# The last layer's output projection as seven-product 2x2 block products

## The chip, the cores and the metric

The kernel runs on one core of a Trainium2 chip. What counts is the time of one execution on the device, in microseconds (us); of several runs the median is given. In the profile the engines are PE (TensorE, the matmuls), DVE (VectorE), ACT (ScalarE), POOL (GpSimd) and SP, which issues the DMAs; PEclk is the clock granted to TensorE, 1.00 being full speed. Each engine carries out its instructions in the order of its own queue.

## The reference

Two encoder layers over 1024 positions of width 1024, all in float32. Only the end of a layer matters here:

```python
y_a = (o_a * jax.nn.silu(z_a)) @ w_attn_proj[l]
y_f = (_fourier_branch(u_f) * jax.nn.silu(z_f)) @ w_fourier_proj[l]
m = (jax.nn.sigmoid(g_a + b_merge[l, 0]) * y_a
     + jax.nn.sigmoid(g_f + b_merge[l, 1]) * y_f)
x = x + m @ w_out[l]
```

The attention branch has 512 channels (`o_a`), `m` and `x` have 1024.

## The kernel before

Activations lie with features on the 128 partitions and the 1024 positions along the free axis, eight tiles of 128 features each. A float32 product is made of three products of a shorter type (`F32R`): every operand is split into an upper part (a copy, rounded) and a lower part (the difference), and upper x upper, upper x lower and lower x upper are added up in PSUM. So a tile of an output of 1024 positions with eight input tiles takes 8 x 2 x 3 = 48 matmuls of 512 columns (`fm`, `mm3`), one with four input tiles 24. Weights are loaded and split on POOL in `wtile` and `split_pool` (L131 the upper, L132 the lower part); activations are split with ACT making the upper and DVE the lower part.

A layer ends with `merge`. Four tiles `og` (what goes into `w_attn_proj`) are loaded and split into `oG` (ACT L797, DVE L798). Then eight tiles t follow: the gate logits `sa` are loaded and put through the sigmoid (ACT L802), the Fourier side's finished summand `mfl` is loaded into one of the three staging buffers (`stage`), TensorE makes `ya` with 24 matmuls, DVE multiplies it from PSUM with the gate (L805) and adds the summand (L806), and ACT L807 and DVE L808 split the sum into the two parts of `mT`. The output projection follows: eight tiles `xo` of 48 matmuls (L165 to L167; in the first tile, where the last tile of `mT` comes late, L187 to L189), DVE adds the residual (L821) and SP stores (L822). The last output tile is added and stored in two halves.

A scheduler sets the order in which each engine's instructions stand, from the order of the code and from estimates; waits are semaphores. PSUM holds two buffers of 1024 columns for the results of `fm`: a tile of `ya` or `xo` can begin when the result two tiles earlier has been read.

## Time and profile before

| | us |
|---|---|
| median of three runs | 1683.38 (1680.42 to 1683.61) |
| the profiled execution | 1679.84 |
| its span (first to last event of the trace) | 1678.1 |
| PE busy | 1647.2 (98%) |
| DVE, ACT, POOL busy | 829.2, 657.6, 730.1 |
| last layer: ya products, output projection | 1541 to 1586, 1586 to 1674 |

The profiled execution is 1.74 us longer than its span and lies below the median of the runs. Busy shares are means over the whole span; what a stage is worth is read from the stage alone, by windows of the trace, and from what ended the waits of the engine that sets its end.

### The profile page before, as it was taken

To read this page: it belongs to the slowest core of one execution; us is meant where nothing else is said; L and a number is where in the kernel's file an instruction comes from. 1 tells how busy PE (TensorE), PEld (TensorE's weight loads), DVE (VectorE), ACT (ScalarE), POOL (GpSimd) and SP (SyncE) were. 2 spreads that over 40 slices of the span, in tenths; PEclk is the share of its full clock that TensorE was granted. 3 is DMA by queue.
4 is the path that set the end of the run, shared out by engine and by line. 5 is a ranking of instruction groups with operands and counts; after the bars stand their busy time and mean duration, and the time that the engine had idled before them with its cause. 6 is when DMAs were issued, how large, how long until landed. Compare 5 with 4: busy or idle time off the path is not lost.

```text
span 1678.1 us, 22508 instructions
## 1 busy us (share of the span) xinstructions
PE 1647.2 (98%) x8374; PEld 1344.1 (80%) x8374; DVE 829.2 (49%) x1358; ACT 657.6 (39%) x1257; POOL 730.1 (44%) x575
## 2 busy tenths in 40 slices
PE   7999999999999999999999999999999999999998
PEld 5888889887777777778878888898777777777887
DVE  7643452334666665465334535424356666654711
ACT  4322321327666666432112223213277666652300
POOL 5622361474454553443254324525644554433531
PEclk9999999999999999999999999999999999999999
DMA  5302330355555553374342023213544555534741
GB/s 193 132 13 71 91 125 32 126 182 186 169 176 199 176 188 132 132 239 162 126 157 63 13 78 121 101 57 132 194 161 176 198 189 176 176 120 173 238 147 75
DMA packets 118366, 234.76 MB, mean 140 GB/s; under 512 B 27888, under 2 KB 48624, under 8 KB 118000
## 3 DMA queue, kind: packets, MB, share of 16 engines
q1 hardware_dynamic: 117904, 228.59, 39.4%
q0 software_dynamic: 352, 4.73, 0.7%
q8 instruction: 66, 1.08, 0.3%
q14 instruction: 44, 0.36, 0.1%
HBM read 116.89 MB, written 49.28 MB: 99 GB/s over the span
## 4 chain that ended last, share of the span: by engine, by line
PE 85%; DMA 4%; issue 3%; DVE 3%; POOL 2%; ACT 2%; SPq 0%; DVEq 0%; POOLq 0%; ACTq 0%
PE pt L714 4%; PE s L165 4%; PE o L718 3%; PE gf L167 3%; PE s L167 3%; PE gf L165 3%; PE xo L167 3%; PE gf L166 3%; PE xo L166 3%; PE xo L165 3%; PE s L166 3%; PE o L720 3%; PE ga L167 3%; PE ga L166 3%; PE ga L165 3%
## 5 line engine op out<-in xcount | busy, mean ns | idle before, releaser
L693 DVE TENSOR_REDUCE nm<-s 128x1 f32<-128x512 f32 x256 | 172.6, 687 | 128.5 <-PE s L167 126.9
L700 ACT ACTIVATE E<-s,nm 128x512 f32<-128x512 f32 x256 | 173.3, 684 | 51.6 <-issue 29.2
L714 PEld LDWEIGHTS pt<-identr,P 128*128 128x128 f32 x1024 | 112.7, 141 | 40.2 <-DMA P<-E 6.8
L131 POOL TENSOR_SCALAR pT<-pf 128x512 fp32r<-128x512 f32 x96 | 59.4, 618 | 176.2 <-ACT pf L725 146.5
L132 POOL TENSOR_TENSOR pT<-pf,pT 128x512 fp32r<-128x512 f32 x96 | 123.8, 1290 | 8.0
L196 DVE TENSOR_TENSOR pT<-pt,pT 128x512 fp32r<-128x512 f32 x160 | 109.2, 684 | 31.5 <-ACT pT L195 30.1
L714 PE MATMUL pt<-identr,P 128*128 128x128 f32 x1024 | 119.9, 239 | 4.7 <-DMA P<-E 4.6
L195 ACT ACTIVATE pT<-pt 128x512 fp32r<-128x512 f32 x160 | 95.5, 598 | 46.1 <-PE pt L714 45.0
L165 PE MATMUL s<-kT,qT 96*128 96x512 f32 x256 | 110.4, 432 | 0.5
L718 PE MATMUL o<-pT,V 128*128 128x512 f32 x256 | 109.7, 428 | 0.0
L720 PE MATMUL o<-pT,V 128*128 128x512 f32 x256 | 106.5, 416 | 1.2 <-POOL pT L132 1.1
L165 PE MATMUL ga<-xg,wga_h 128*128 128x512 f32 x256 | 103.1, 403 | 0.0
L166 PE MATMUL ga<-xg,wga_h 128*128 128x512 f32 x256 | 102.0, 399 | 0.0
L167 PE MATMUL ga<-xg,wga_l 128*128 128x512 f32 x256 | 101.7, 397 | 0.0
L165 PE MATMUL gf<-xg,wgf_h 128*128 128x512 f32 x256 | 101.0, 395 | 0.0
L166 PE MATMUL s<-kT,qT 96*128 96x512 f32 x256 | 101.0, 394 | 0.0
L167 PE MATMUL gf<-xg,wgf_l 128*128 128x512 f32 x256 | 100.9, 394 | 0.0
L166 PE MATMUL gf<-xg,wgf_h 128*128 128x512 f32 x256 | 100.9, 394 | 0.0
L167 PE MATMUL s<-kT,qT 96*128 96x512 f32 x256 | 96.5, 396 | 0.0
L725 ACT ACTIVATE pf<-pt 128x512 f32<-128x512 f32 x96 | 57.4, 598 | 97.3 <-PE pt L714 92.7
L167 PE MATMUL xo<-mT,wo_l 128*128 128x512 f32 x224 | 87.9, 392 | 0.0
L166 PE MATMUL xo<-mT,wo_h 128*128 128x512 f32 x224 | 87.9, 392 | 0.0
(335 smaller groups left out, 4269.2 us busy)
## 6 DMA issues: line engine op xcount, KB each, us to landing
P<-E SPq DMA_DIRECT2D x256, 256.0 KB, 2.3
kv_d<-KV SPq DMA_DIRECT2D x16, 640.0 KB, 2.9
KVh<-kv_d SPq DMA_DIRECT2D x16, 640.0 KB, 4.9
wgf_r<-in_w_fm SPq DMA_DIRECT2D x16, 512.0 KB, 3.5
mf_d<-sgf SPq DMA_DIRECT2D x16, 512.0 KB, 3.3
wga_r<-in_w_fm SPq DMA_DIRECT2D x16, 512.0 KB, 3.6
ga_d<-sga SPq DMA_DIRECT2D x16, 512.0 KB, 3.0
sa<-ga_d SPq DMA_DIRECT2D x16, 512.0 KB, 4.1
```

Of the source, the lines that this page charges most:

```text
L131: nc.gpsimd.tensor_scalar(hi, src, 1.0, 1.0, op0=ALU.mult, op1=ALU.mult)
L132: nc.gpsimd.tensor_tensor(lo, src, f(hi), op=ALU.subtract)
L165: self.nc.tensor.matmul(out, ah, bh, start=(i == 0), stop=False)
L166: self.nc.tensor.matmul(out, ah, bl, start=False, stop=False)
L167: self.nc.tensor.matmul(out, al, bh, start=False, stop=(i == n - 1))
L195: nc.scalar.activation(hi, ps, AF.Copy)
L196: nc.vector.tensor_tensor(lo, ps, f(hi), op=ALU.subtract)
L693: nc.vector.tensor_reduce(nm2[:, kc:kc + 1], s_ps, axis=AX.X, op=ALU.max)
L700: nc.scalar.activation(e, halves[kc], AF.Exp, bias=nm, accum_out=sum_e[:, h, t, kc:kc + 1])
L714: nc.tensor.transpose(tp[:, j * P:(j + 1) * P].bitcast(F32R), u["P"][j][k // 4][:, (k % 4) * P:(k % 4 + 1) * P], self.identr)
L718: nc.tensor.matmul(u["o"], u["V"][:, kk, :], q[0], start=(u["n"] == 0), stop=False)
L720: nc.tensor.matmul(u["o"], u["V"][:, kk, :], q[1], start=False, stop=(u["n"] == ST))
```

## The change

Layer 0 keeps `merge`. The last layer gets `merge_last`, which makes the same output projection in blocks. For each pair of output tiles (j = 0 to 3) the weights are two block rows and two block columns (the input tiles 0 to 3 and 4 to 7), and the positions two halves of 512. A 2x2 block product takes eight products of blocks; here it takes seven, of sums and differences of blocks. A product of blocks is four input tiles x 3 = 12 matmuls of 512 columns, so that a pair of output tiles takes 7 x 12 = 84 matmuls instead of 96.

On the side of `m` the operands are the blocks M1 (lower half of tiles 0 to 3), M2 (tiles 4 to 7) and the mixtures XA and XB, made from tile k and tile k + 4 as soon as both are there: therefore the ya products run in the order 0, 4, 1, 5, 2, 6, 3, 7, and the weights of tiles k and k + 4 are loaded and split as one pair of 1024 columns (`pair`). The gate logits go through the three staging buffers, as the summands do (`gal`, `mfl`). The lower parts of XA and XB are issued one tile later (`tail`): XA's on DVE, XB's on POOL for k = 0 and 1 and on DVE for k = 2 and 3.

`stream` runs the 28 products. On the weights' side POOL makes four sums or differences for each j, and ACT and DVE split the operands (`split_fast`). Behind each product ACT or DVE takes the result out of PSUM or combines it with an earlier one, and POOL adds residuals (`base`). The PSUM buffers are those of a new pool (`px`), six of 512 columns, in place of the old two of 1024. The buffers for the further weight tiles (`R`) are in a pool that opens when the pool of `oG` has closed.

Lines of the changed kernel that are named below: L138 and L139 are `split_fast` (ACT, DVE), L133 and L134 `split_pool`; L875 is the multiplication of ya with the gate, L876 the addition of the summand, L879 the difference of the halves of a tile, L892 to L894 the differences with the other tile, L895 and L896 the copies to XA and XB, L897 their lower parts; L933 to L936 the four weight sums, L952 `base`, L970 to L972 the matmuls of a step, L980 the copy of a first result (`c`).

```diff
-    def merge(self, l, og3, x_ctx, res_d, out_d):
+    def merge(self, l, og3, x_ctx, res_d):
...
                 ps = self.fm_late(w, mT, f"xo{t}") if t == 0 else self.fm(w, mT, KD, f"xo{t}")
-                dst = out_d[t] if last else self.x1_d[t]
-                for cs in (slice(0, 512), slice(512, S)) if last and t == KD - 1 else (slice(0, S),):
-                    nc.vector.tensor_tensor(xr[:, cs], ps[:, cs], xr[:, cs], op=add)
-                    nc.sync.dma_start(dst[:, cs], xr[:, cs])
...
+    def merge_last(self, l, og3, x_ctx, res_d, out_d):
...
+        self.psum(f"pm{l}")
...
+        with ExitStack() as ctx:
+            mp = ctx.enter_context(tc.tile_pool(name=f"m{l}", bufs=1, side=xs))
+            sp = ctx.enter_context(tc.tile_pool(name=f"sa{l}", bufs=1, side=xs))
+            M1, M2, XA, XB = [[mp.tile([P, 4, n], F32R, name=f"{name}{j}") for j in range(2)]
+                              for name, n in (("M1", 512), ("M2", S), ("XA", S), ("XB", S))]
+            cut = lambda x, cs: [y[:, :, cs] for y in x]
+            self.X = {B11: M1, B21: cut(M2, lo), B22: cut(M2, hi), T1: cut(XA, lo), T3: cut(XA, hi), T4: cut(XB, lo), T2: cut(XB, hi)}
+            self.sa_p, self.cp = sp, None
+            mixed = {}
+            with tc.tile_pool(name=f"og{l}", bufs=1, side=os) as op_:
+                oG = [op_.tile([P, 4, S], F32R, name=f"oG{j}") for j in range(2)]
+                for t in range(4):
+                    o = self.stage(self.og_d[t], f"og{t}") if t < 3 else og3
+                    nc.scalar.activation(oG[0][:, t, :], o, AF.Copy)
+                    nc.vector.tensor_tensor(oG[1][:, t, :], o, f(oG[0][:, t, :]), op=sub)
+
+                def pair(k):
+                    raw = self.wp.tile([P, S], F32, tag="raw", name=f"wa{k}_r")
+                    w = [self.wp.tile([P, S], F32R, tag=n, name=f"wa{k}_{n}") for n in ("hi", "lo")]
+                    for j, cs in enumerate((lo, hi)):
+                        nc.sync.dma_start(raw[:, cs], io["w_ap"][l, k + 4 * j])
+                    self.split_pool(raw, *w)
+                    for j, cs in enumerate((lo, hi)):
+                        W[k + 4 * j] = [x[:, cs].rearrange("p (k m) -> p k m", k=4) for x in w]
+
+                W = {}
+                pair(0)
+                tail = []
+                for t in (0, 4, 1, 5, 2, 6, 3, 7):
+                    k = t % 4
+                    ga = self.stage(self.ga_d[t], f"gal{t}")
+                    mf = self.stage(self.mf_d[t], f"mfl{t}")
+                    ps = self.fm(W.pop(t), oG, 4, f"ya{t}")
+                    if t < 3:
+                        pair(t + 1)
+                    if t + 1 == KD:
+                        stream = self.stream(l, res_d, out_d)
+                        next(stream)
+                    nc.scalar.activation(ga, ga, AF.Sigmoid, bias=self.bm[:, l, 0, t:t + 1])
+                    sa = mixed[t] = sp.tile([P, S], F32, tag="sa", bufs=4, name=f"sa{t}")
+                    nc.vector.tensor_tensor(sa, ps, ga, op=mult)
+                    nc.vector.tensor_tensor(sa, sa, mf, op=add)
+                    if t < 4:
+                        self.split_fast(sa[:, lo], M1[0][:, k], M1[1][:, k])
+                        nc.gpsimd.tensor_tensor(sa[:, lo], sa[:, hi], sa[:, lo], op=sub)
+                    else:
+                        self.split_fast(sa, M2[0][:, k], M2[1][:, k])
+                    for do in tail:
+                        do()
+                    tail = []
+                    if t < 4:
+                        continue
+                    if t + 1 == KD:
+                        self.psum(f"px{l}")
+                        next(stream)
+                        next(stream)
+                    y = mixed[k]
+                    nc.vector.tensor_tensor(y[:, hi], sa[:, hi], y[:, hi], op=sub)
+                    nc.gpsimd.tensor_tensor(sa[:, hi], sa[:, hi], y[:, lo], op=sub)
+                    nc.gpsimd.tensor_tensor(sa[:, lo], sa[:, lo], sa[:, hi], op=sub)
+                    nc.scalar.activation(XA[0][:, k], y, AF.Copy)
+                    nc.scalar.activation(XB[0][:, k], sa, AF.Copy)
+                    low = lambda e, X, x, k: e.tensor_tensor(X[1][:, k], x, f(X[0][:, k]), op=sub)
+                    tail = [lambda k=k, y=y: low(nc.vector, XA, y, k), lambda k=k, sa=sa: low(nc.gpsimd if k < 2 else nc.vector, XB, sa, k)]
+                for do in tail:
+                    do()
+            self.cp = ctx.enter_context(tc.tile_pool(name=f"xo{l}", bufs=1, side=os))
+            for _ in stream:
+                pass
+
+    def stream(self, l, res_d, out_d):
+        nc, io = self.nc, self.io
+        add, sub = ALU.add, ALU.subtract
+        J = KD // 2
+        steps = [(0, 0), (1, 0), (0, 2), (1, 2)]
+        steps += [(j, i) for j in range(J) for i in ((1, 3, 4, 5, 6) if j < 2 else range(7))]
+        loads = [s for s in steps if s[1] < 2]
+        last = {(j, r): max(steps.index((j, i)) for i in ((0, 1, 2) if r == 0 else (1, 5))) for j in range(J) for r in range(2)}
+        R, ops, sums, banks, tiles, xr, pair = {}, {}, {}, {}, {}, {}, {}
+        early, nb = 2, 4
+
...
+        def prep(n):
+            if n >= len(steps):
+                return
+            pump(n)
+            j, i = steps[n]
+            half = lambda r, h: R[j, r][:, h * 512:h * 512 + 512]
+            if i == 1:
+                s1, s2, s3, s4 = sums[j] = [self.cp.tile([P, 512], F32, tag=f"s{m}", name=f"S{m}_{j}") for m in range(1, 5)]
+                nc.gpsimd.tensor_tensor(s1, half(1, 0), half(1, 1), op=add)
+                nc.gpsimd.tensor_tensor(s2, s1, half(0, 0), op=sub)
+                nc.gpsimd.tensor_tensor(s3, half(0, 0), half(1, 0), op=sub)
+                nc.gpsimd.tensor_tensor(s4, half(0, 1), s2, op=sub)
+            if i in (0, 2, 5):
+                src = half(i == 5, i != 0)
+            else:
+                src = sums[j][(None, 1, None, 2, 0, None, 3)[i]]
+            if n % 2 == 0:
+                pair[n] = pair[n + 1] = [self.wp.tile([P, S], F32R, tag=t, name=f"A{t}{n}") for t in ("hi", "lo")]
+            cs = slice(n % 2 * 512, n % 2 * 512 + 512)
+            ops[n] = [x[:, cs] for x in pair.pop(n)]
+            self.split_fast(src, *ops[n])
+            pump(n + 1)
+
...
+        for n in range(AHEAD):
+            prep(n)
+        yield
+        V = nc.vector
+        lo, hi = slice(0, 512), slice(512, S)
+        for n, (j, i) in enumerate(steps):
+            prep(n + AHEAD)
+            tag = ("b1", "bx", "b1", "bx", "bz", "bx", "bz")[i]
+            fresh = i in (0, 1, 4)
+            if fresh:
+                banks[j, tag] = self.ps.tile([P, 512], F32, tag=tag, bufs=2, name=f"{tag}_{j}")
+            b = banks[j, tag]
+            ah, al = ops.pop(n)
+            bh, bl = self.X[i]
+            for k in range(4):
+                ks = slice(k * P, k * P + P)
+                nc.tensor.matmul(b, ah[:, ks], bh[:, k, :], start=(fresh and k == 0), stop=False, skip_group_check=True)
+                nc.tensor.matmul(b, ah[:, ks], bl[:, k, :], start=False, stop=False, skip_group_check=True)
+                nc.tensor.matmul(b, al[:, ks], bh[:, k, :], start=False, stop=(k == 3), skip_group_check=True)
+            if i in (0, 1 if j > 1 else 2):
+                tiles[j, int(i == 0)] = self.sa_p.tile([P, S], F32, tag="sa", bufs=4, name=f"c{j}{int(i == 0)}")
+            for m in range(2):
+                if i == (((2, 1), (0, 2))[j > 1][m]):
+                    xr[j, m] = self.stage(res_d[2 * j + m], f"xr{j}{m}")
+            a, t, ra, rt = tiles.get((j, 0)), tiles[j, 1], xr.get((j, 0)), xr.get((j, 1))
+            if i == 0:
+                nc.scalar.activation(t[:, lo], b, AF.Copy)
+            elif i == 1:
+                V.tensor_tensor(a[:, hi], b, t[:, lo], op=add)
+                base(a, hi, ra)
+            elif i == 2:
+                V.tensor_tensor(a[:, lo], b, ra[:, lo], op=add)
+                store(j, 0, a, lo)
+            elif i == 3:
+                V.tensor_tensor(t[:, hi], b, t[:, lo], op=add)
+            elif i == 4:
+                V.tensor_tensor(t[:, hi], b, t[:, hi], op=add)
+                base(t, hi, rt)
+                store(j, 1, t, hi)
+            elif i == 5:
+                V.tensor_tensor(t[:, lo], b, t[:, lo], op=add)
+                base(t, lo, rt)
+                store(j, 1, t, lo)
+            else:
+                V.tensor_tensor(a[:, hi], b, a[:, hi], op=add)
+                store(j, 0, a, hi)
+            yield
 
```

The order of instructions on DVE, from the second-last pair of ya products to the last multiplication of the stage. The names are those of the code with a running number (`M11` and `M21` the lower parts of M1 and M2, `XA1` and `XB1` those of XA and XB). Before:

```order
L805 TENSOR_TENSOR sa5_14754<-ya5_14765,sa5_14754 128x1024
L806 TENSOR_TENSOR sa5_14754<-sa5_14754,mfl5_14757 128x1024
L808 TENSOR_TENSOR mT1_14539<-sa5_14754,mT0_14538 128x1024
L805 TENSOR_TENSOR sa6_14794<-ya6_14805,sa6_14794 128x1024
L806 TENSOR_TENSOR sa6_14794<-sa6_14794,mfl6_14797 128x1024
L808 TENSOR_TENSOR mT1_14539<-sa6_14794,mT0_14538 128x1024
L805 TENSOR_TENSOR sa7_14834<-ya7_14845,sa7_14834 128x1024
L806 TENSOR_TENSOR sa7_14834<-sa7_14834,mfl7_14837 128x1024
L808 TENSOR_TENSOR mT1_14539<-sa7_14834,mT0_14538 128x1024
```

After:

```order
L892 TENSOR_TENSOR sa2_14775<-sa6_14813,sa2_14775 128x512
L139 TENSOR_TENSOR M21_14539<-sa6_14813,M20_14538 128x1024
L897 TENSOR_TENSOR XA1_14541<-sa2_14775,XA0_14540 128x1024
L875 TENSOR_TENSOR sa3_14853<-ya3_14827,gal3_14823 128x1024
L876 TENSOR_TENSOR sa3_14853<-sa3_14853,mfl3_14825 128x1024
L897 TENSOR_TENSOR XB1_14543<-sa6_14813,XB0_14542 128x1024
L139 TENSOR_TENSOR M11_14537<-sa3_14853,M10_14536 128x512
L875 TENSOR_TENSOR sa7_14901<-ya7_14865,gal7_14861 128x1024
L139 TENSOR_TENSOR Alo2_14911<-wx00_14890,Ahi2_14910 128x512
```

Between two multiplications stood an addition and one lower part; now the multiplication of ya7 (L875 with `sa7`) stands behind lower parts of M2, XA, XB and M1 and a difference.

The order on POOL at the end of the ya products. Before:

```order
L132 TENSOR_TENSOR wa6_l_14801<-wa6_r_14799,wa6_h_14800 128x512
L131 TENSOR_SCALAR wa7_h_14840<-wa7_r_14839 128x512
L132 TENSOR_TENSOR wa7_l_14841<-wa7_r_14839,wa7_h_14840 128x512
L131 TENSOR_SCALAR wo0_h_14881<-wo0_r_14880 128x1024
L132 TENSOR_TENSOR wo0_l_14882<-wo0_r_14880,wo0_h_14881 128x1024
L131 TENSOR_SCALAR wo1_h_14940<-wo1_r_14939 128x1024
```

After:

```order
L897 TENSOR_TENSOR XB1_14543<-sa5_14728,XB0_14542 128x1024
L879 TENSOR_TENSOR sa2_14775<-sa2_14775 128x512
L893 TENSOR_TENSOR sa6_14813<-sa6_14813,sa2_14775 128x512
L894 TENSOR_TENSOR sa6_14813<-sa6_14813 128x512
L879 TENSOR_TENSOR sa3_14853<-sa3_14853 128x512
L933 TENSOR_TENSOR S1_0_14965<-wx01_14957 128x512
L935 TENSOR_TENSOR S3_0_14967<-wx00_14890,wx01_14957 128x512
L934 TENSOR_TENSOR S2_0_14966<-S1_0_14965,wx00_14890 128x512
L936 TENSOR_TENSOR S4_0_14968<-wx00_14890,S2_0_14966 128x512
L893 TENSOR_TENSOR sa7_14901<-sa7_14901,sa3_14853 128x512
L894 TENSOR_TENSOR sa7_14901<-sa7_14901 128x512
```

POOL had splits of weights alone there; now the differences and a lower part of XB stand there, and the four sums for j = 0 ahead of the differences of the last tile.

The order on ACT behind the last ya. Before:

```order
L807 ACTIVATE mT0_14538<-sa5_14754 128x1024
L802 ACTIVATE sa6_14794<-sa6_14794,bm_284 128x1024
L807 ACTIVATE mT0_14538<-sa6_14794 128x1024
L802 ACTIVATE sa7_14834<-sa7_14834,bm_284 128x1024
L807 ACTIVATE mT0_14538<-sa7_14834 128x1024
```

After:

```order
L138 ACTIVATE M20_14538<-sa7_14901 128x1024
L980 ACTIVATE c01_14927<-b1_0_14914 128x512
L895 ACTIVATE XA0_14540<-sa3_14853 128x1024
L896 ACTIVATE XB0_14542<-sa7_14901 128x1024
L980 ACTIVATE c11_14944<-b1_1_14931 128x512
L138 ACTIVATE Ahi4_14973<-S2_0_14966 128x512
```

The copies `c01` and `c11`, which read the first two results of the stream, stand between the copies for the last pair's operands; `c11` is behind the copy to XB.

The order of SP's DMA issues around the loads of `og`. Before:

```order
L145 DMA wa2_r_14639<-in_w_ap 128x512
L126 DMA og0_14540<-og_d_73 128x1024
L126 DMA og1_14544<-og_d_73 128x1024
L126 DMA og2_14548<-og_d_73 128x1024
L478 DMA ga_d_71<-sga7_14471 128x1024
```

After:

```order
L855 DMA wa2_r_14682<-in_w_ap 128x512 x2
L128 DMA og0_14549<-og_d_73 128x1024
L128 DMA og1_14553<-og_d_73 128x1024
L128 DMA og2_14557<-og_d_73 128x1024
L480 DMA ga_d_71<-sga7_14471 128x1024
```

One load of weights ahead of the `og` loads became two.

## Rows read from the trace of the kernel before

**Rows 1.** The page: busy time of each engine, its share of the span, instructions.

```profile
PE 1647.2 (98%) x8374; PEld 1344.1 (80%) x8374; DVE 829.2 (49%) x1358; ACT 657.6 (39%) x1257; POOL 730.1 (44%) x575
```

**Rows 2.** Busy time by stage: window, length, PE, PEld, DVE, ACT, POOL, PEclk, DMA, GB/s.

```profile
1541.00:1586.00 45.00, 44.52 (x191) 35.54 (x191) 29.67 (x22) 13.63 (x13) 19.17 (x15) 1.00 0.72 242
1586.00:1674.00 88.00, 87.35 (x386) 72.00 (x384) 15.56 (x13) 2.49 (x3) 25.05 (x14) 1.00 0.33 119
```

**Rows 3.** Timeline of DVE at the program's end: start, duration, line, operation, tiles [idle before].

```profile
1662.51 1.22 DVE L821 TENSOR_TENSOR xr<-xo,xr 128x1024 f32<-128x1024 f32 x1 [9.66 <-PE xo L167]
1673.39 1.29 DVE L821 TENSOR_TENSOR xr<-xo,xr 128x512 f32<-128x512 f32 x2 [9.65 <-PE xo L167]
```

**Rows 4.** Groups of DVE by shape, last stage: busy us, mean ns of one | idle before.

```profile
L821 DVE TENSOR_TENSOR xr<-xo,xr 128x512 f32<-128x512 f32 x2 | 1.3, 684 | 9.7 <-PE xo L167 9.7
```

**Rows 5.** Timeline of DVE in the ya stage.

```profile
1561.89 1.22 DVE L806 TENSOR_TENSOR sa<-sa,mfl 128x1024 f32<-128x1024 f32 x1
...
1582.70 2.59 DVE L806 TENSOR_TENSOR sa<-sa,mfl 128x1024 f32<-128x1024 f32 x1
1586.42 1.85 DVE L808 TENSOR_TENSOR mT<-sa,mT 128x1024 fp32r<-128x1024 f32 x1 [1.13 <-ACT mT L807]
1588.19 1.21 DVE L805 TENSOR_TENSOR sa<-ya,sa 128x1024 f32<-128x1024 f32 x1
```

**Rows 6.** Timeline of POOL in the same stretch.

```profile
1581.81 2.40 POOL L132 TENSOR_TENSOR wo_l<-wo_r,wo_h 128x1024 fp32r<-128x1024 f32 x1
1586.15 1.05 POOL L131 TENSOR_SCALAR wo_h<-wo_r 128x1024 fp32r<-128x1024 f32 x1 [1.94 <-PE ya L166]
1587.28 3.25 POOL L132 TENSOR_TENSOR wo_l<-wo_r,wo_h 128x1024 fp32r<-128x1024 f32 x1
```

**Rows 7.** Timeline of DVE at the program's start, queue full.

```profile
11.01 2.06 DVE L225 TENSOR_TENSOR acc<-acc,sq 128x1024 f32<-128x1024 f32 x1
...
16.35 2.06 DVE L225 TENSOR_TENSOR acc<-acc,sq 128x1024 f32<-128x1024 f32 x1
18.33 3.40 DVE L218 SCALAR_TENSOR_TENSOR xg<-x,ng,xg 128x1024 fp32r<-128x1024 f32 x1
```

**Rows 8.** Timeline of POOL in the same stretch.

```profile
15.32 2.02 POOL L131 TENSOR_SCALAR wu_h<-wu_r 128x1024 fp32r<-128x1024 f32 x1
17.42 3.22 POOL L132 TENSOR_TENSOR wu_l<-wu_r,wu_h 128x1024 fp32r<-128x1024 f32 x1
```

**Rows 9.** Groups of POOL by shape, 100 to 1000 us.

```profile
L132 POOL TENSOR_TENSOR pT<-pf,pT 128x512 fp32r<-128x512 f32 x48 | 61.9, 1290 | 4.0
...
L132 POOL TENSOR_TENSOR wga_l<-wga_r,wga_h 128x1024 fp32r<-128x1024 f32 x8 | 19.2, 2397 | 1.7 <-PE aa L167 1.1
...
L131 POOL TENSOR_SCALAR wu_h<-wu_r 128x1024 fp32r<-128x1024 f32 x8 | 8.5, 1058 | 23.2 <-PE xo L166 15.3 <-PE u_c L284 4.0 <-DMA wu_r<-in_w_u 3.9
```

**Rows 10.** Timeline of POOL, first split of the last layer's wa.

```profile
1528.62 0.69 POOL L131 TENSOR_SCALAR wa_h<-wa_r 128x512 fp32r<-128x512 f32 x1 [2.15 <-PE ga L166]
1529.39 1.30 POOL L132 TENSOR_TENSOR wa_l<-wa_r,wa_h 128x512 fp32r<-128x512 f32 x1
```

**Rows 11.** Timeline of SP's DMA queue, same stretch: duration of the issues, last loads of og.

```profile
1530.72 0.33 SPq L145 DMA_DIRECT2D wa_r<-in_w_ap  x1
1531.15 7.01 SPq L126 DMA_DIRECT2D og<-og_d  x3
```

**Rows 12.** Timeline of PE: a matmul that waited for the split of og.

```profile
1542.62 0.50 PE L166 MATMUL ya<-oG,wa_h 128*128 128x512 f32 x1 [0.48 <-DVE oG L798]
```

**Rows 13.** Groups of ACT, ya stage: busy us, mean ns.

```profile
L807 ACT ACTIVATE mT<-sa 128x1024 fp32r<-128x1024 f32 x7 | 7.4, 1063 | 28.7 <-DVE sa L806 28.7
```

**Rows 14.** Timeline of PE at the program's start: two matmuls behind waits.

```profile
21.79 0.51 PE L284 MATMUL ab<-wu_h,xg 128*128 128x512 f32 x1 [2.23 <-DVE xg L218]
...
37.12 0.50 PE L284 MATMUL ab<-wu_h,xg 128*128 128x512 f32 x1 [2.27 <-DVE xg L218]
```

**Rows 15.** Busy time by stretch, as rows 2: behind the first of these waits.

```profile
24.00:25.00 1.00, 1.00 (x3) 0.80 (x3) 1.00 (x2) 1.00 (x1) 0.00 (x0) 0.50 0.43 44
```

More of the change, by code (lines that the diff above doesn't have):

```diff
@@ L36 @@
 ORD = "SFVV"
+AHEAD = 2
+B11, T2, B21, T3, T1, T4, B22 = range(7)
 SEQ = ('u z0 T F0 z1 C0 G0 F1 z2 C1 F2 G1 C2 F3 z3 M C3 G2 G3', 'u z0 T F0 z1 C0 G0 F1 z2 C1 F2 G1 C2 F3 z3 G2 M C3 G3')
@@ L808, in merge @@
                 nc.vector.tensor_tensor(mT[1][:, t, :], sa, f(mT[0][:, t, :]), op=sub)
-        last = l + 1 == L
         n_ctx = ExitStack()
-        if not last:
-            xp = n_ctx.enter_context(tc.tile_pool(name=f"x{l + 1}", bufs=1, side=os))
-            xg = [xp.tile([P, KD, S], F32R, name=f"xg{l + 1}{j}") for j in range(2)]
+        xp = n_ctx.enter_context(tc.tile_pool(name=f"x{l + 1}", bufs=1, side=os))
+        xg = [xp.tile([P, KD, S], F32R, name=f"xg{l + 1}{j}") for j in range(2)]
         with tc.tile_pool(name=f"xo{l}", bufs=1, side=xs) as op_:
@@ new lines, in stream, with pump, store, base @@
+    def stream(self, l, res_d, out_d):
[8 more added lines that the diff above has]
+        early, nb = 2, 4
+        def pump(n):
+            while len(R) < (len(loads) if self.cp else early) and (len(R) < early + nb or last[loads[len(R) - nb]] < n):
+                j, i = loads[len(R)]
+                if len(R) < early:
+                    R[j, i] = self.wp.tile([P, S], F32, tag="raw", name=f"wx{j}{i}")
+                else:
+                    R[j, i] = self.cp.tile([P, S], F32, tag="R", bufs=nb, name=f"wx{j}{i}")
+                nc.sync.dma_start(R[j, i], io["w_o"][l, 2 * j + i])
+        def prep(n):
[20 more added lines that the diff above has]
+            pump(n + 1)
+        def store(j, m, x, cs):
+            nc.sync.dma_start(out_d[2 * j + m][:, cs], x[:, cs])
+        def base(x, cs, r):
+            nc.gpsimd.tensor_tensor(x[:, cs], x[:, cs], r[:, cs], op=add)
+        for n in range(AHEAD):
+            prep(n)
+        yield
+        V = nc.vector
+        lo, hi = slice(0, 512), slice(512, S)
+        for n, (j, i) in enumerate(steps):
[36 more added lines that the diff above has]
+                store(j, 1, t, lo)
+            else:
+                V.tensor_tensor(a[:, hi], b, a[:, hi], op=add)
+                store(j, 0, a, hi)
+            yield
```

22 lines of the change are left out of this document (14 added, 8 removed).

## The prediction, made before the changed kernel ran

> **What bounds the kernel now.** I read the page's busy table first: TensorE is busy 98% of the span, and no other engine reaches half of it [rows 1]. The table by stage repeats that for the two stages that the change touches: 44.52 of 45.00 us while the last layer's ya products run, and 87.35 of 88.00 us in the output projection, both at full granted clock [rows 2]. So matmuls set the end there, and a matmul taken away is worth its pitch, as long as the other engines keep up. The timeline of VectorE gives that pitch: its L821, one for each output tile, starts at 1662.51 and at 1673.39, 10.88 us for 48 matmuls, 0.2267 us each [rows 3]. The profiled execution (1679.84 us, span 1678.1 with 1.74 around it) is 3.54 us under the median of the three runs, 1683.38. I make the sum on the profiled execution and put the same difference on the median. 0.2% is 3.4 us, about what a measurement of this kernel can tell from no change.
>
> **What is removed.** Eight tiles of 48 matmuls become 28 steps of 12: 336 instead of 384, and 48 x 0.2267 = 10.9 us less for TensorE. At the very end, two additions of 512 columns after the last matmul (1.29 us [rows 3]) become one (0.68 [rows 4]): 0.6 less. Together **-11.5 us**. The weight splits of the projection leave POOL for ACT and VectorE, which idle through most of that stage [rows 2].
>
> **What is added, and where it lies.** Nearly all of it lies in the 45 us of the ya stage and in the first steps behind it: differences of tiles, lower parts of four operands instead of one, sums of weight blocks. Alone, each engine would fit. They do not run alone. In the timelines of VectorE and POOL, an instruction of VectorE with two SBUF inputs and an instruction of POOL never run at once. POOL's L132 holds 1581.81 to 1584.21, and L806, started at 1582.70, takes 2.59 instead of the 1.22 of the undisturbed L806 at 1561.89: it ends 1.08 after POOL has. L808 at 1586.42 takes 1.85 and ends 1.07 after POOL's L131 (1586.15 for 1.05); POOL's L132 at 1587.28 takes 3.25 instead of 2.40 and ends 2.26 after L808 [rows 5, 6]. L805, which has an input in PSUM, takes its 1.21 at 1588.19, in the middle of that L132 [rows 5]. At the start of the program both engines have a full queue, and there VectorE's two operations and POOL's two repeat every 16.35 - 11.01 = 5.34 us: 1.08 + 1.08 + 0.92 + 2.26 [rows 7, 8]. That is what I charge: 1.08 for 1024 columns on VectorE, 0.54 for 512 (0.68 less the same 0.14), and on POOL 0.92 and 2.26 for the two halves of a split of 1024, 1.15 for a subtraction of 512 (1.29 less 0.14) [rows 4, 9].
>
> The Trainium skill ("SBUF — State Buffer", section "Who interferes with whom") has a rule for this: a VectorE instruction with two SBUF inputs contends with a GpSimd instruction that reads SBUF, under an exclusive lock, and one with at most one SBUF input does not. The rows agree with it for 1024 columns on VectorE; by the rule the 512-column operations, of which the rows show no pair, are held as well, and the stalls below follow, without them the first rival.
>
> **Start of the stage.** The first split of wa becomes that of a pair, 1024 wide: 1.05 + 2.40 instead of 0.69 + 1.30, so it ends 1.4 later [rows 9, 10]. SP's next weight load stood right behind it, at 1530.72, with the three loads of og behind that at 1531.15 [rows 11]; now two weight loads stand there, 0.4 more. TensorE already waits for the og split (0.48 us [rows 12]), so this is paid in full: **+1.9**.
>
> **The backlog up to the last ya.** The first product of the stream takes PSUM banks that the last ya held, and so waits for its multiplication (L875), which stands in VectorE's queue behind all that was put in before it. Between the end of ya0 and that multiplication the order has on VectorE 14 operations of 1024 with two SBUF inputs (seven additions, three lower parts of M2, three of XA, one of XB) and nine of 512 (four lower parts of M1, three differences, two weight splits): 14 x 1.08 + 9 x 0.54 = 20.0. On POOL: two pair splits, nine subtractions of 512 and two lower parts of XB, 2 x 3.18 + 9 x 1.15 + 2 x 2.26 = 21.2. Together 41.2 us that only one of the two can use at a time. To it come stretches in which neither can go on: the first multiplication (1.2), a first copy on ACT (about 0.6, estimated as half of 1.06), and three times the copy to XB (1.06 [rows 13]), since VectorE or POOL stands at the lower part of XB while ACT makes its upper part from what POOL has just subtracted: 3.2. That is 46.2. TensorE needs from the end of ya0 to the end of the last ya seven tiles of 24 at 0.2333 (191 in 44.52 us [rows 2]), less the seven matmuls of the second tile that stand ahead of ya0's last: 39.2 - 1.6 = 37.6. The difference is **+8.6**, part of it as waits of ya3 and ya7 for their banks (each needs the multiplication two tiles earlier), the rest ahead of the first stream product; the multiplication itself adds **+1.3**. In the kernel before none of this is seen: the lower part at the end of the ya stage is met by other matmuls.
>
> **Behind the last ya.** From that multiplication on, TensorE has 1.3 and then three steps of 2.72, 9.5 us. Its fourth step adds to the bank that ACT's copy c11 must have read first, and c11 stands in ACT's queue behind the last copy to XB, which waits for POOL's L894. Ahead of that stand POOL's L879, the four weight sums (whose load starts only when the last ya has freed the room) and L893, L894: 7 x 1.15 = 8.05; and between them VectorE's addition, lower parts of M2 and XA, difference and two weight splits: 3 x 1.08 + 3 x 0.54 = 4.9. With the two copies (1.06 and about 0.6) c11 is done 14.6 us after the multiplication: **+5.1**, of which less than 1 is a wait for M2's lower part.
>
> **Clock.** Of two waits of 2.2 to 2.3 us at the program's start one was followed by a granted clock of 0.50 (the lower level, 1.2 GHz), at matmuls 0.43 us apart, and one was not [rows 14, 15]; eight or nine matmuls at 0.2 us more is 1.7. A wait of about 6 us is longer than both, so I take one such fall, **+1.7**, with none and two as bounds (0 and 3.4).
>
> **Sum.** 1.9 + 8.6 + 1.3 + 5.1 + 1.7 = 18.6 against 11.5: +7.1. The profiled execution would be 1686.9, the median **1690.5**. What is left open is above all hand-offs between engines that the count leaves out (up to 3 more) and the second fall of the clock (1.7): up to 1695.5. Later steps cost nothing more: each lasts 2.72 us, and asks of VectorE and POOL some 2 us of it.
>
> **Rivals.** First, on the other side: the exclusion does not hold for pairs of 512, which are what the change adds most of. Then POOL's nine subtractions and VectorE's nine small operations run beside each other, and only 15.1 + 6.4 + 4.5 = 26 us of 1024-wide work must take turns, well inside 37.6. What stays is the start (1.9), the multiplication with one lower part ahead of it (2.5) and a c11 that waits for POOL alone: 7 x 1.29 + 1.66 = 10.7 against 9.5, so 1.2. 5.6 - 11.5 = -5.9: a median of 1677.5, faster. For it speaks that the rows show no such pair; against it that POOL's half of each excluded pair is the same operation as in the rows. It decides from stalls below 11.5 - 3.4 = 8.1 us. Second: the stalls are there but overlap. What waits ahead of the first stream product gives POOL and VectorE time to clear, so that c11 costs 1.5 instead of 5.1, and the hand-offs to ACT are covered by the other engine (3.2 less): 1.9 + 5.4 + 1.3 + 1.5 = 10.1 without a fall of the clock, -1.4, 1682: no change. For it speaks that POOL has waits of its own in which VectorE can go on; against it that both queues are in order, and the sums stand ahead of L893. Third: all is hidden, only the start stays: -9.6, 1673.8; that needs both queues to be empty when the last ya ends, and the count of 41.2 against 37.6 speaks against it.
>
> **Numbers.** The forecast 0.70, the first rival 0.14, the second 0.13, the third 0.03. So slower 0.70, same 0.13, faster 0.17. The range goes from 1678, about the first rival, to 1697: the upper bound of the sum and the 1.6 us by which single runs stand apart.
>
> **What would show it.** Right: TensorE waits before ya3, ya7 and the first b1 that are released by VectorE's L875, and before the fourth stream step by ACT's L980; VectorE's L876, L139 and POOL's L893 to L897 at up to twice their time alone in the ya stage; steps 2.72 us apart behind that. Wrong: 512-wide operations of VectorE at 0.68 beside a running POOL instruction, or a first stream product right behind the last ya. If the waits are there and the time is still lower, the pitch of the stream's matmuls is not 0.2267.

## The result, and the profile after

The changed kernel takes 1692.54 us, the median of 6 runs (1688.73 to 1697.52), against 1682.43 for the kernel before (6 runs, 1680.42 to 1684.09): a ratio of 1.0062, 95% interval 1.005 to 1.0075. It is slower by some 10 us; 1690.5 was forecast, with a range of 1678 to 1697. The profiled execution took 1691.49 us, 11.65 more than that of before; +7.1 was forecast, and by the medians it is +10.1.

The busy table of the changed kernel's page (span 1689.7 us):

```profile
PE 1644.2 (97%) x8326; PEld 1338.3 (79%) x8326; DVE 876.1 (52%) x1411; ACT 681.5 (40%) x1297; POOL 762.7 (45%) x593
```

Against [rows 1] TensorE has 48 matmuls and 3.0 us of busy time less (the busy time includes matmuls at the lower clock, of which there are now more), and VectorE, ScalarE and POOL have 47, 24 and 33 us more. By stage (columns as in [rows 2]), the ya products with the waits behind them, the first steps of the stream, and the rest of it:

```profile
1541.00:1600.00 59.00, 47.85 (x192) 36.75 (x192) 44.90 (x34) 25.41 (x28) 33.33 (x16) 0.97 0.60 196
1600.00:1640.00 40.00, 34.77 (x134) 27.70 (x135) 24.73 (x27) 10.12 (x16) 27.52 (x18) 0.88 0.42 152
1640.00:1686.00 46.00, 46.00 (x203) 37.75 (x202) 22.44 (x30) 9.19 (x16) 18.64 (x13) 1.00 0.28 98
```

In 1541 to 1600 TensorE is busy for 47.85 of 59 us, where [rows 2] had 44.52 of 45.00; VectorE and POOL together show 78 us of busy time in these 59, the time in which one is held by the other among it. From 1640 on TensorE runs without a gap. The waits of TensorE between 1541 and 1640, by what released them (in total, times, longest):

```profile
PE b L970 <- DVE sa L875: 7.3, 1, 7.3
PE b L970 <- ACT c L980: 3.3, 1, 3.3
PE ya L167 <- DVE sga L474: 2.7, 1, 2.7
PE ya L167 <- DVE sa L875: 2.5, 2, 2.4
```

The first ya (2.7) belongs to the start of the stage. The other places are those that were forecast: ya3 and the first product of the stream (behind VectorE's L875) and its fourth step (behind ScalarE's L980); the wait of ya7, forecast too, is 0.18 us. On the timeline of PE they are:

```profile
1542.52 0.47 PE L167 MATMUL ya<-oG,wa_hi 128*128 128x512 f32 x1 [2.73 <-DVE sga L474]
...
1581.16 0.47 PE L167 MATMUL ya<-oG,wa_hi 128*128 128x512 f32 x1 [2.37 <-DVE sa L875]
...
1601.88 0.77 PE L970 MATMUL b<-M,Ahi 128*128 128x512 f32 x1 [7.31 <-DVE sa L875]
...
1615.73 0.50 PE L970 MATMUL b<-M,Ahi 128*128 128x512 f32 x1 [3.35 <-ACT c L980]
```

Then the mechanism, in the timelines of VectorE and of POOL:

```profile
1559.84 2.72 DVE L892 TENSOR_TENSOR sa<-sa,sa 128x512 f32<-128x512 f32 x1
...
1575.32 3.42 DVE L139 TENSOR_TENSOR M<-sa,M 128x1024 fp32r<-128x1024 f32 x1
...
1600.52 1.22 DVE L875 TENSOR_TENSOR sa<-ya,gal 128x1024 f32<-128x1024 f32 x1
...
1604.15 1.77 DVE L892 TENSOR_TENSOR sa<-sa,sa 128x512 f32<-128x512 f32 x1
```

```profile
1558.60 3.40 POOL L134 TENSOR_TENSOR wa_lo<-wa_r,wa_hi 128x1024 fp32r<-128x1024 f32 x1
...
1574.95 2.71 POOL L134 TENSOR_TENSOR wa_lo<-wa_r,wa_hi 128x1024 fp32r<-128x1024 f32 x1
...
1600.68 1.27 POOL L879 TENSOR_TENSOR sa<-sa 128x512 f32<-128x512 f32 x1 [3.03 <-DVE M L139]
...
1603.65 1.72 POOL L933 TENSOR_TENSOR S<-wx 128x512 f32<-128x512 f32 x1 [1.71 <-DMA wx<-in_w_o]
```

L892, 512 columns wide, takes 2.72 instead of 0.68 and ends at 1562.56, 0.56 after POOL's L134 (1558.60 + 3.40); the lower part of M2 at 1575.32 takes 3.42, as L218 did in [rows 7]. L892 at 1604.15 ends 0.55 after POOL's L933 at 1603.65, and both are 512 wide: the pair that the rows of before did not have. L875 at 1600.52, with one input in PSUM, takes its 1.22 although POOL's L879 runs beside it from 1600.68 on.

To place the loss I cut both profiled executions at the same four events: the end of the gate logits' matmuls (the first ya's start less the wait ahead of it), the first multiplication of the ya stage, the first matmul behind the last ya, and the last matmul. The first multiplication of after is this row; before it stood at 1548.76:

```profile
1552.53 1.22 DVE L875 TENSOR_TENSOR sa<-ya,gal 128x1024 f32<-128x1024 f32 x1 [4.39 <-PE ya L169]
```

| stretch | before | after | more | forecast |
|---|---|---|---|---|
| end of ga's matmuls to the first multiplication | 1539.64 to 1548.76: 9.12 | 1539.79 to 1552.53: 12.74 | 3.6 | 1.9 |
| to the first matmul behind the last ya | to 1586.13: 37.37 | to 1601.88: 49.35 | 12.0 | 8.6 + 1.3 |
| three steps, to the fourth | 3 x 2.72 = 8.16 | to 1615.73: 13.85 | 5.7 | 5.1 |
| 25 steps, to the last matmul's end | 25 x 2.72 + 0.17 = 68.2 | to 1686.01: 70.28 | 2.1 | 1.7 (clock) |
| 48 matmuls and the end of the span | | | -10.9 - 1.1 | -11.5 |

The sum is 23.4 - 12.0 = 11.4; with the 0.15 by which the first event is later it is the 11.6 by which the spans differ. (Steps of before are set in at the pitch of [rows 3].)

### The profile page after: what moved, and what is told of

Same layout as the page of the kernel before. It is cut to its first block, busy times and chain, and to the rows that moved or that the text cites. A ratio compares the mean times of both kernels' runs of the same rounds, so it can differ in the third digit from the quotient of the medians.

```text
span 1689.7 us, 22565 instructions
## 1 busy us (share of the span) xinstructions
PE 1644.2 (97%) x8326; PEld 1338.3 (79%) x8326; DVE 876.1 (52%) x1411; ACT 681.5 (40%) x1297; POOL 762.7 (45%) x593
## 3 DMA queue, kind: packets, MB, share of 16 engines
q8 instruction: 66, 1.08, 0.3%
## 4 chain that ended last, share of the span: by engine, by line
PE 82%; DVE 5%; DMA 4%; POOL 3%; issue 3%; ACT 3%; SPq 0%; POOLq 0%; ACTq 0%; DVEq 0%
PE pt L716 4%; PE s L167 4%; PE gf L169 3%; PE gf L168 3%; PE gf L167 3%; PE o L720 3%; PE s L169 3%; PE o L722 3%; PE s L168 3%; PE ga L169 3%; PE ga L168 3%; PE ga L167 3%; DMA P<-E 2%; PE aa L167 2%; PE c L501 2%
## 5 line engine op out<-in xcount | busy, mean ns | idle before, releaser
L133 POOL TENSOR_SCALAR pT<-pf 128x512 fp32r<-128x512 f32 x96 | 59.3, 618 | 176.4 <-ACT pf L727 146.7
L134 POOL TENSOR_TENSOR pT<-pf,pT 128x512 fp32r<-128x512 f32 x96 | 123.8, 1289 | 8.0
L500 PE MATMUL c<-wc_h,xg 128*128 128x256 f32 (+1 forms) x256 | 73.5, 290 | 0.5 <-ACT wc_h L160 0.4
L501 PE MATMUL c<-wc_l,xg 128*128 128x256 f32 (+1 forms) x256 | 73.5, 288 | 0.3 <-DVE wc_l L161 0.3
```

The source lines that it names most:

```text
L134: nc.gpsimd.tensor_tensor(lo, src, f(hi), op=ALU.subtract)
L501: nc.tensor.matmul(ps, xg[0][:, k, ts], wl[:, k, :], start=False, stop=False)
```

## Experiments

All changes are to the changed kernel, if nothing else is said. Its runs lie up to 8.8 us apart. Part of that arises ahead of the ya stage: in the profiled executions of the changed kernel and of the nine variants below, the matmuls of ga end anywhere from 1538.69 to 1543.51. So beside the medians I give, for one profiled execution each, the stretch from the first multiplication to the end of the span: 129.34 us before (1548.76 to 1678.1), 137.17 after (1552.53 to 1689.7).

**All on VectorE.** POOL's share of the ya stage goes to VectorE (ScalarE makes the upper parts of the splits; the split of the first pair and the weight sums of the stream stay on POOL):

```diff
-                        nc.gpsimd.tensor_tensor(sa[:, lo], sa[:, hi], sa[:, lo], op=sub)
+                        nc.vector.tensor_tensor(sa[:, lo], sa[:, hi], sa[:, lo], op=sub)
...
-                    nc.gpsimd.tensor_tensor(sa[:, hi], sa[:, hi], y[:, lo], op=sub)
-                    nc.gpsimd.tensor_tensor(sa[:, lo], sa[:, lo], sa[:, hi], op=sub)
+                    nc.vector.tensor_tensor(sa[:, hi], sa[:, hi], y[:, lo], op=sub)
+                    nc.vector.tensor_tensor(sa[:, lo], sa[:, lo], sa[:, hi], op=sub)
...
-low(nc.gpsimd if k < 2 else nc.vector, XB, sa, k)
+low(nc.vector, XB, sa, k)
...
-                    self.split_pool(raw, *w)
+                    (self.split_fast if k else self.split_pool)(raw, *w)
```

> POOL's whole share of the ya stage (the three differences of a tile pair, the lower parts of XB, the splits of the second to fourth pair of wa) goes to VectorE, the upper parts of those splits to ScalarE; TensorE's 8000 rows are the same. VectorE gets nine more subtractions of 512, and up to five more of 1024, 11 to 12 us of its own time. Turn-taking theory: what counts is the sum of both engines' two-input work, and a subtraction costs 0.54 on VectorE against 1.15 on POOL, a lower part 1.08 against 2.26, a split 1.08 against 3.18, so the sum falls by about 12 us; waits before ya3 and ya7 go, the wait before the first stream product falls from 7.5 to about 6, that before the fourth step from 3.5 to about 1: median about 1683, 9 to 10 under the changed kernel. Rival, VectorE's own queue is too long and POOL runs beside it for nothing: 11 us more in that queue, the wait before the first product grows by about as much: 1700 or more.

Measured: 1684.74 us (ratio to before 1.0018, 1.0006 to 1.003), 7.8 less than the changed kernel; the stretch is 126.89, 10.3 less. The waits of TensorE in this kernel, and then two groups of VectorE's operations from 1541 to 1640 (busy us, mean ns) in this kernel and in the changed one:

```profile
PE b L970 <- DVE sa L875: 5.8, 1, 5.8
...
PE b L970 <- ACT c L980: 1.5, 1, 1.5
```

```profile
L876 DVE TENSOR_TENSOR sa<-sa,mfl 128x1024 f32<-128x1024 f32 x8 | 9.8, 1220 | 0.0
...
L892 DVE TENSOR_TENSOR sa<-sa,sa 128x512 f32<-128x512 f32 x4 | 2.7, 684 | 0.0
```

```profile
L876 DVE TENSOR_TENSOR sa<-sa,mfl 128x1024 f32<-128x1024 f32 x8 | 11.7, 1468 | 0.2
...
L892 DVE TENSOR_TENSOR sa<-sa,sa 128x512 f32<-128x512 f32 x4 | 6.5, 1628 | 0.2
```

The same operations take 1220 and 684 ns instead of 1468 and 1628. VectorE has more to do and is done earlier, and the wait ahead of the stream falls from 7.3 to 5.8 us, that ahead of the fourth step from 3.3 to 1.5. The rival, a VectorE queue that is too long with POOL beside it, is out.

**Work for POOL that nobody waits for.** Two kernels on top of the last one. In the first, POOL subtracts parts of M1 and M2 into a tile that is never read; in the second it fills that tile instead, behind a copy of two columns that ties it to the same place:

```diff
+                        nc.gpsimd.tensor_tensor(scrap[:, lo], f(M1[0][:, k]), f(M1[1][:, k]), op=sub)
...
+                        nc.gpsimd.tensor_tensor(scrap, f(M2[0][:, k]), f(M2[1][:, k]), op=sub)
```

```diff
+                        self.blank(scrap, f(M1[1][:, k, :2]), 1)
...
+                        self.blank(scrap, f(M2[1][:, k, :2]), 2)
...
+    def blank(self, x, y, n):
+        self.nc.gpsimd.tensor_scalar(x[:, :2], y, 1.0, 1.0, op0=ALU.mult, op1=ALU.mult)
+        for _ in range(n):
+            self.nc.gpsimd.memset(x, 0.0)
```

> The kernel with everything on VectorE (1684.7), in which POOL stands idle through the ya stage, and eight subtractions more on POOL: the upper less the lower part of M1 (512, four times) and of M2 (1024, four times), into a tile that nobody reads and on which nobody waits. They take POOL 4 x 1.29 + 4 x 2.40 = 14.8 us; the order of all other engines is the same, instruction by instruction. Turn-taking theory: they hold VectorE's two-input operations for what they last, less what falls beside multiplications from PSUM or into idle time: 8 to 13.5 us longer, 1693 to 1698. Rival, POOL's work was slow in the chain but held nobody: nobody depends on these, 1684.7.

> The same, but what POOL gets at those eight places reads almost nothing: a copy of two columns, and then one (M1) or two (M2) fills of the 1024-column tile with zero, twelve fills in all, each about 0.9 us by estimate from a 128-column one in the trace that took 0.20. Again nobody waits for them and all other engines keep their order. If the turns are about reading SBUF, the fills hold nobody: 1684.7, at most 1 more for the small copies. If any work of POOL holds VectorE, about 10 us longer, 1694.

Measured: 1691.64 us with the subtractions (ratio 1.0057, 1.004 to 1.0074), 1684.01 with the fills (1.0015, 1.0005 to 1.0024). With the subtractions: one of them on POOL's timeline, VectorE's addition beside it, two groups of VectorE, and the wait ahead of the stream:

```profile
1580.55 2.71 POOL L884 TENSOR_TENSOR scrap<-M,M 128x1024 f32<-128x1024 f32 x1 [6.45 <-DVE M L139]
```

```profile
1580.92 3.42 DVE L877 TENSOR_TENSOR sa<-sa,mfl 128x1024 f32<-128x1024 f32 x1
```

```profile
L877 DVE TENSOR_TENSOR sa<-sa,mfl 128x1024 f32<-128x1024 f32 x7 | 12.9, 1838 | 0.0
...
L881 DVE TENSOR_TENSOR sa<-sa 128x512 f32<-128x512 f32 x4 | 5.3, 1317 | 0.0
```

```profile
PE b L973 <- DVE sa L876: 13.8, 1, 13.8
```

The addition (here L877) at 1580.92 ends 1.08 after POOL's subtraction. Over seven additions the mean has gone from 1220 to 1838 ns: two of them were held so, the other five took 1.21 or 1.22. The difference of a tile's halves (L881) takes 1317 on the mean, and the wait has gone from 5.8 to 13.8 us. With the fills, a group and a row of POOL, then a row and a group of VectorE:

```profile
L911 POOL MEMSET scrap<- 128x1024 f32 x12 | 11.5, 954 | 0.7
...
1564.81 1.97 POOL L911 MEMSET scrap<- 128x1024 f32 x2
```

```profile
1566.06 1.22 DVE L877 TENSOR_TENSOR sa<-sa,mfl 128x1024 f32<-128x1024 f32 x1
...
L877 DVE TENSOR_TENSOR sa<-sa,mfl 128x1024 f32<-128x1024 f32 x8 | 9.8, 1219 | 0.0
```

There are 11.5 us of fills, and all eight additions take their time alone, the one at 1566.06 although it starts while a fill runs (to 1566.78). So it is not that POOL works, but that it reads SBUF while VectorE has two inputs there: POOL's subtractions, on which nobody depends, cost 7 us, a little under the 8 to 13.5 that I expected. Some ran in part beside a multiplication, as one at 1565.37 did beside L876, and the wait ahead of the fourth step fell from 1.5 to 0.7.

By the Trainium skill ("SBUF — State Buffer", section "Who interferes with whom") a VectorE instruction with two SBUF inputs contends with a GpSimd instruction that reads SBUF, and not with one that only writes it. These two runs agree with both halves of that sentence: 3.42 us for the addition beside a subtraction, 1.22 beside the fills.

**Banks of their own.** The stream's first results go to PSUM buffers that the ya products never held:

```diff
-                        self.psum(f"px{l}")
...
-                banks[j, tag] = self.ps.tile([P, 512], F32, tag=tag, bufs=2, name=f"{tag}_{j}")
+                banks[j, tag] = self.mm_ps(f"{tag}_{j}")[:, :512] if tag == "bz" else self.ps.tile([P, 512], F32, tag=tag, bufs=2, name=f"{tag}_{j}")
```

> The stream's first PSUM buffers (b1, bx) are banks that the ya products never held; only bz shares the old ones. Nothing else is changed, but the scheduler moves a few instructions. Turn-taking theory: the first product then waits for the lower part of M1, which stands one place ahead of the last multiplication in VectorE's queue, so only the multiplication itself (1.3) and what overlaps behind it is won: 1.3 to 3.5 off, median 1689 to 1691. Rival, the hand-over of the banks is the cause of the 7.5 us: 6 off or more, 1686.5 or less.

Measured: 1689.66 us (ratio 1.0053, 1.0034 to 1.0072), 2.9 less than the changed kernel; the stretch is 134.03, 3.1 less. The hand-over of the banks is the smaller part of the 7.3 us. The stream now starts right behind the last ya, but at the last tile of its first step it waits 2.67 us for the upper part of M1 and then 0.84 for the lower one. That upper part stands in ScalarE's queue behind the copy to XB, which waits for POOL's subtraction: what makes the larger part is the lateness of this chain.

**A filled wait.** Fifteen matmuls whose result nobody reads stand ahead of the fourth step, where TensorE would wait:

```diff
+            if n == 3:
+                self.idle(self.X[B11], 15, "f2")
...
+            self.nc.tensor.matmul(ps, x[0][:, 0, :P], x[0][:, 0, :512], start=(i == 0), stop=(i == n - 1), skip_group_check=True)
```

> 15 matmuls whose result nobody reads (15 x 0.2267 = 3.4 us) stand ahead of the fourth stream step, in the 3.5 us that TensorE waits there; the order of all else is the same. If the wait is what lets the clock fall, the eight matmuls at 0.43 behind it become 0.23 ones and 1.6 us go: median 1691. If the fall has another cause, or the waits are not as long in the other runs, they cost nothing or add up to 3.4: 1692.5 to 1696.

Measured: 1691.75 us (ratio 1.006, 1.0037 to 1.0082), which alone tells nothing; the stretch is 135.50, 1.7 less, and from the start of the fourth step to the end of the span it is 72.40 us (1614.10 to 1686.5) instead of 73.97 (1615.73 to 1689.7). Timeline of PE there:

```profile
1610.12 3.56 PE L912 MATMUL f<-M 128*128 128x512 f32 x15
1614.10 0.50 PE L981 MATMUL b<-M,Ahi 128*128 128x512 f32 x1 [0.41 <-ACT c L991]
...
1614.90 0.40 PE L981 MATMUL b<-M,Ahi 128*128 128x512 f32 x1
1615.13 0.39 PE L982 MATMUL b<-M,Ahi 128*128 128x512 f32 x1
```

The wait behind the 15 matmuls is 0.41, and the matmuls that follow are 0.23 us apart, as at the full clock. In the changed kernel the granted clock fell to the lower of its two levels, 0.50, at three places (columns as in [rows 2]):

```profile
1582.00:1586.00 4.00, 4.00 (x12) 3.13 (x11) 0.27 (x1) 2.56 (x4) 2.83 (x2) 0.57 0.82 262
1602.00:1606.00 4.00, 4.00 (x10) 3.13 (x11) 4.00 (x5) 1.06 (x1) 2.35 (x2) 0.50 1.02 406
1617.00:1619.00 2.00, 2.00 (x6) 1.57 (x5) 1.25 (x3) 0.00 (x0) 1.27 (x1) 0.50 0.04 8
```

**The start.** The two weight loads of the third pair, which stand ahead of the og loads in SP's queue, are issued by ScalarE:

```diff
-                        nc.sync.dma_start(raw[:, cs], io["w_ap"][l, k + 4 * j])
+                        (nc.scalar if k == 2 else nc.sync).dma_start(raw[:, cs], io["w_ap"][l, k + 4 * j])
```

> The two loads for the third pair of wa go to ScalarE's DMA queue, so that SP's queue issues the og loads without waiting for the wide split. Theory: the whole chain from the first multiplication to the copy c11 begins earlier by what the start loses, so the end moves by the same: TensorE's first ya matmuls wait some 2 us less, median 1690 to 1691. Rival: the waits further on take up whatever the start gives, because loads of the gate logits set them: no change, 1692.5.

Measured: 1688.94 us (ratio 1.0045, 1.003 to 1.006), 3.6 less than the changed kernel and more than the 1.5 to 2.5 expected. The first ya's matmul and the first multiplication:

```profile
1542.02 0.47 PE L167 MATMUL ya<-oG,wa_hi 128*128 128x512 f32 x1 [0.88 <-DVE sga L474]
```

```profile
1550.86 1.23 DVE L875 TENSOR_TENSOR sa<-ya,gal 128x1024 f32<-128x1024 f32 x1 [4.39 <-PE ya L169]
```

From 1541.14 to 1550.86 it is 9.72, where it was 12.74: 3.0 of the 3.6 that the start lost are back, and the end has moved with them. (In this profiled execution the clock did not fall behind ya3 and the fourth step. Behind ya3 that won nothing: ya7 then waited 1.76 us instead of 0.18. Behind the fourth step it did: from there to the end it is 72.41 us instead of 73.97, and the stretch is 135.74. So some of the 3.6 may be the clock's.)

**No mixing.** The kernel leaves out the differences between tiles and the operands made of them; the products take M2 instead:

```diff
-            self.X = {B11: M1, B21: cut(M2, lo), B22: cut(M2, hi), T1: cut(XA, lo), T3: cut(XA, hi), T4: cut(XB, lo), T2: cut(XB, hi)}
+            self.X = {B11: M1, B21: cut(M2, lo), B22: cut(M2, hi), T1: cut(M2, lo), T3: cut(M2, hi), T4: cut(M2, lo), T2: cut(M2, hi)}
...
-                        nc.gpsimd.tensor_tensor(sa[:, lo], sa[:, hi], sa[:, lo], op=sub)
...
-                    y = mixed[k]
...
-                    nc.scalar.activation(XB[0][:, k], sa, AF.Copy)
```

> Left out: the differences between tiles and the operands XA and XB with their parts; the products that used them take M2 instead. Matmuls, weights, weight sums, stores and the order of the stream stay. If the 48 matmuls are worth their pitch and all that was lost was lost to the mixing, what is left of the losses is the start (3.5), the last multiplication ahead of the first product (1.5) and a short wait behind it (0.6): 1682.5 - 11.5 + 5.6 = 1676.6. Rival, the stream itself costs (its weight sums, its splits or the result's way out hold TensorE up, or its matmuls are slower): 1681 or more.

Measured: 1675.64 us (ratio 0.996, 0.9947 to 0.9974); one wait is left in the stream:

```profile
1593.23 0.48 PE L961 MATMUL b<-M,Ahi 128*128 128x512 f32 x1 [1.41 <-DVE sa L875]
```

From its start, which this row shows, to the end of the span the stream takes 80.67 us, and the projection before took 91.97 from 1586.13 on: 11.3 less, where 12.0 is what pitch and end give. So the 48 matmuls are worth nearly what the pitch says, and the stream, its weight sums among it, hides: what was lost behind the start of the stage was lost to the mixing. (The start itself was longer still in this execution: the first ya waited 5.17 us.)

**Together.** The first sets L893, L894, the lower parts of XB and the later splits on VectorE (POOL keeps L879), with own banks and the start's loads on ScalarE's queue. The second has L879 on VectorE too, and takes the first four steps in two pairs:

```diff
+            if n < 4:
+                if n % 2 == 0:
+                    prep(n + 2)
+                    prep(n + 3)
+                    mm(n, (0, 1, 2))
+                    mm(n + 1, (0, 1, 2))
+                b = mm(n, (3,))
```

> Three edits together: VectorE instead of POOL for L893, L894, the lower parts of XB and the later pair splits (POOL keeps L879, the first split and the weight sums); banks of its own for the stream's first results; the loads of the third pair of wa on ScalarE's DMA queue. If the causes found are separate and add up: 10 from the first, 1 to 2 of the 3 from the second (the queue is shorter, so less is left to win), 3 from the third: 1678 to 1679, under the kernel before by about 4. Rival, each edit gives back the same waits, so that together they are not better than all on VectorE alone: 1683 to 1685.

> As the one before, but L879 too is on VectorE, and the stream's first four steps run in two pairs in which the last tile's three matmuls of both steps come behind the first three tiles' of both, so that the last tile's lower parts may come 4 us later. If what is left in front of the first product is the last tile alone, another 0.5 to 2 us: 1676.5 to 1678. If VectorE's queue as a whole is late, nothing: 1678 to 1679.

Measured: 1678.29 us (ratio 0.9983, 0.9969 to 0.9996) and 1676.87 (0.9969, 0.9957 to 0.9982). Both are faster than the kernel before, by 0.2 and 0.3%, and by the ratios faster than the changed one by some 13 and 16 us. The largest wait of TensorE that is left is 3.9 us in the first (for ScalarE's copy of M2's last tile) and 2.6 in the second (for a copy of a first result). By the ratios the three single edits gained 0.44, 0.09 and 0.17%, together 0.70%, and the first combination, which leaves one of the moves out, 0.79%: within the intervals the causes add up. In the second the stretch is 125.99 us (1547.21 to 1673.2).

## Why the prediction was right, point by point

**The sum.** Every loss came out larger than its term, by 1.7, 2.1, 0.6 and 0.4 us, and the saving by 0.5: in the profiled executions 11.4 instead of 7.1. That the median still lies within 2.1 us of the forecast is luck in part: the forecast was put on a median of three runs, 1683.38, where six runs give 1682.43. (Its upper end has a slip: 1690.5 + 3 + 1.7 is 1695.2, not 1695.5.)

**The saving** was sized right: 10.9 by pitch, and the end of the span gave 1.1 instead of 0.6. The run without mixing, with 11.3 of 12.0, shows that little else in the stream eats it.

**The start** was right in its place and too small: 3.6 for 1.9. SP issues the og loads at 1533.27, 2.1 later than in [rows 11]; that is the part that was forecast. The rest is the first of these loads. Two rows of after (SP's queue, ScalarE), and ScalarE's row of before:

```profile
1533.27 8.85 SPq L128 DMA_DIRECT2D og<-og_d  x3
```

```profile
1539.27 1.06 ACT L848 ACTIVATE oG<-og 128x1024 fp32r<-128x1024 f32 x1 [11.57 <-DMA og<-og_d]
```

```profile
1535.49 1.06 ACT L797 ACTIVATE oG<-og 128x1024 fp32r<-128x1024 f32 x1 [3.35 <-DMA og<-og_d]
```

ScalarE has this tile 6.00 us after the issue, where before it was 4.34 (1535.49 less 1531.15). Two weight loads instead of one were issued just ahead of it; with these on ScalarE's queue it is 4.04. The last og load needs the buffer that the first tile's split frees (L849 ends at 1541.78, the load is issued at 1541.80), and so it is late by about the sum of both. The wider split of the second pair is not what makes it. It does hold VectorE's lower part of the second og tile (2.81 instead of 1.22), but with everything on VectorE that split is not on POOL, and the start is as long: 12.70 against 12.74. In the seven kernels with all these loads on SP's queue it is 11.74 to 15.10, in the three with two of them on ScalarE's 8.52 to 9.72. Among these three, those with the later splits on VectorE have 8.52 each: there the hold shows, with about 1.2.

**The backlog** was the term that decided, and held: 9.9 forecast, 12.0 measured. The count of 41.2 us of work that takes turns, plus 5.0 of gaps, put the last multiplication's end 47.5 after the first one's start; it came at 1601.74, 49.2 after it. The two timelines bear out both parts: between the starts of these multiplications POOL, or VectorE with two inputs in SBUF, is at work for 43.2 us, and neither is for 4.8, which are the first multiplication (1.26), the first copy (0.76), two of the three copies to XB (1.16 and 1.12) and 0.5 of small gaps.

**Behind the last ya**, 5.1 forecast, 5.7 measured, by the chain named: POOL's last subtraction (it ends at 1614.10), the copy to XB, the copy c11:

```profile
1614.13 1.06 ACT L896 ACTIVATE XB<-sa 128x1024 fp32r<-128x1024 f32 x1 [5.55 <-POOL sa L894]
1615.10 0.58 ACT L980 ACTIVATE c<-b 128x512 f32<-128x512 f32 x1
```

**The clock** was right in its sum by luck. I took one fall, behind the longest wait. There were three, but the first two stand ahead of a wait that another engine ends: ya7 waits for L875 and the fourth step for L980 whether TensorE arrives early or late, so the slow matmuls only took up waiting time (the kernel with the other start, without the first fall, waits the longer for ya7). The third, behind the fourth step, has nothing behind it to hide in, and the filled wait gives back 1.6 of it. So the step that did not hold is that the fall behind the longest wait is paid in full; what counts is whether a wait for another engine follows. For the second fall this is read from the timeline alone: no run was without it.

**The rivals.** The first, that pairs of 512 do not exclude each other, fell with L892 at 1604.15 and with the two kernels that load POOL. The second, that the stalls overlap, fell with 5.7 for the copy c11. The third, all hidden but the start, 1673.8, is not what this kernel does: it takes leaving out the mixing to come near to it (1675.64).

## What to carry to other kernels

Where VectorE's operations have two inputs in SBUF and POOL's read SBUF too, add up this work as if one engine did it, and ask of each operation on which of the two it takes the shorter turn: here a subtraction of 512 costs 0.54 on VectorE and 1.15 on POOL, so that moving work from POOL to the busier VectorE made the kernel 8 us faster. Give POOL work that does not read SBUF, or place it beside VectorE's reads of PSUM. A slow stretch of an engine counts only if no wait for another engine follows it.
